# Output weights of four FFNs: their low halves from a negated copy and a transfer that adds, in place of a subtraction on VectorE

## The chip, the cores and the metric

The kernel runs on one core of one Trainium2 chip. Times are microseconds of device time of one execution of the whole program, and the median of several executions is compared. The profile is of one further execution.

## What is computed

A trunk of two layers over 256 context tokens and 512 latent tokens of width 1024. Each layer is a half-step SwiGLU FFN, a token mixer (differential attention in the first layer, grouped-query attention in the second) and another half-step FFN, each between two RMS norms and modulated by vectors that are made from the conditioning vectors `c` and `c_ctx`. The part that the change touches is the second matrix of the FFN, `w_out` of 2816 x 1024:

```python
def swiglu(h, w_in, w_out):
    gate, up = jnp.split(h @ w_in, 2, axis=-1)
    return (jax.nn.silu(gate) * up) @ w_out
```

All inputs are float32. The output is the latent stream, 512 x 1024.

## The kernel before, in words

**Products.** Every float32 operand is split in two float32r tiles: `hi` is a rounded copy (ScalarE, line 103, `nc.scalar.copy`), `lo` is what the rounding left, `src - hi` (VectorE, line 104). A product is three matmuls that add up in one PSUM bank: hi x hi, hi x lo, lo x hi. Weights come by a DMA on SyncE's queue into one of four `stage` buffers (line 129), and are split into a tile `wh` and a tile `wl`; there are six of each (`wtile`), used by all weights of the kernel.

**An FFN.** `ffn` runs four times: three times over all six tiles of 128 tokens ("wide"), and once over the four latent tiles. It first makes the 22 chunks of 128 columns of `silu(gate) * up`, each of which goes to DRAM (`gd`, line 468). In a wide FFN `chunk` does this with seven block products instead of eight, in an order of VectorE, ScalarE, GpSimd and TensorE that is written out by hand. Then comes w_out: `operand(c)` loads chunk c back (tile `gr`, or a `stage` buffer for the first three), splits it into `gx` tiles, and loads and splits the 128 x 1024 block c of `w_out`. The 22 operands are used in groups of 3, 3, 3, 3, 3, 2 and 5 (`GROUPS`): for each tile of tokens and each half of 512 columns, `project_half` runs three matmuls for each operand of the group into a bank `y_ps` (line 423; four banks), and `add_y` adds the bank to `y` in SBUF (ScalarE copies it for the first group, line 412; VectorE adds it after that, line 414). While one group runs, the operands of the next are made. The operands of the first group are made inside the last chunk of the first matrix (`prepare` and `finish_operands`, called by `chunk`). `w_out_last` runs the last group and, tile by tile, the norms that follow (`Finish`: GpSimd's lines 369, 97 and 99, VectorE's 382 and 388); there the order of VectorE, ScalarE and GpSimd is the program's.

**Beside it.** Between these steps, `Fillers` let VectorE make the modulation vectors of later layers from `ada_w` (lines 181 and 185), whose blocks also come through the `stage` buffers.

**What sets the order.** Outside of the orders written by hand, a planner sorts each engine's instructions before the program runs, by priority and by the time at which it expects operands and free tiles; that holds for TensorE in the whole of w_out, and for all engines in the groups but the last. On the chip each engine then runs its instructions in that order and waits where an operand is not there.

The names of the change: `operand` (line 670), `load_w` (line 112), which it called, `split` (line 102), `stage` and `wtile`.

Of the kernel before, what the change touches and what calls it, by code (L numbers as in the profile page):

```python
# [11 lines left out]
F32R = mybir.dt.float32r  # L12
AF = mybir.ActivationFunctionType
ALU = mybir.AluOpType
# [5 lines left out]
P = 128  # L20
D = 1024
# [38 lines left out]
def trunk(ctx: ExitStack, tc: tile.TileContext, a: dict, out: bass.AP):  # L60
    nc = tc.nc
# [40 lines left out]
    def split(hi, lo, src):  # L102
        nc.scalar.copy(hi, src)  # L103
        nc.vector.tensor_tensor(out=lo, in0=src, in1=raw(hi), op=ALU.subtract)  # L104

    def stage():
        return wp.tile([P, 1024], F32, tag="stage", name="stage", bufs=NSTAGE)

    def wtile(which):
        return wp.tile([P, 1024], F32R, tag="w" + which, name="w" + which, bufs=6)  # L110

    def load_w(src, dims, tiles=None):

        n = 1
        for d in dims:
            n *= d
        names = "abc"[: len(dims)]
        spec = {k: v for k, v in zip(names, dims)}

        def view(t):  # L120
            t = t[:, :n]
            return t.rearrange(f"p ({' '.join(names)}) -> p {' '.join(names)}", **spec) if len(dims) > 1 else t

        st = stage()
        if len(dims) == 3:
            for i in range(dims[0]):
                nc.sync.dma_start(out=view(st)[:, i], in_=src[:, i])
        else:
            nc.sync.dma_start(out=view(st), in_=src)
        hi, lo = tiles or (wtile("h"), wtile("l"))  # L130
        split(hi[:, :n], lo[:, :n], st[:, :n])
        return view(hi), view(lo)
# [310 lines left out]
    def ffn(ctx, l, s, tiles, place, fin, vectors, opening=None):  # L443
# [6 lines left out]
        w2 = a["ffn_w_out"][l, s]  # L450
# [205 lines left out]
        def two_tiles(which):  # L656
            if which == "k":
                return [ep.tile([P, 768], F32R, tag=f"kt{i}", name="gx", bufs=2) for i in range(2)]
            pool, n = (xp, 4) if which == "t" else (ep, 2)
            x = pool.tile([P, 2, 768], F32R, tag=which, name="gx", bufs=n)  # L660
            return x[:, 0, :], x[:, 1, :]
# [3 lines left out]
        def load_operand(c):  # L665
            r = stage() if c < GROUPS[0] else ep.tile([P, 768], F32, tag="pl", name="gr", bufs=4)
            nc.sync.dma_start(out=r[:, :nt], in_=gd[c])
            return r

        def operand(c, r=None):  # L670
            r = r or load_operand(c)
            gh, gl = two_tiles(next(slots))
            split(gh[:, :nt], gl[:, :nt], r[:, :nt])
            w = load_w(w2[c * P : (c + 1) * P, :], (D,))
            return (lambda t: gh[:, pos[t] : pos[t] + P], lambda t: gl[:, pos[t] : pos[t] + P]), w

        def w_out(ops, first):
# [29 lines left out]
        def prepare(n):  # L707
            if n < len(run):
                run[n].weights()
            else:  # L710
                rows.extend(load_operand(c) for c in range(2))
                ops.append(operand(0, rows[0]))
# [7 lines left out]
        def finish_operands(n):  # L720
            if n < len(run):
                run[n].summed()
            else:
                ops.append(operand(1, rows[1]))
                ops.extend(operand(c) for c in range(2, GROUPS[0]))
# [31 lines left out]
        if wide:  # L757
            run[0].load()
            with tc.manual_schedule(engines={ET.DVE, ET.Activation, ET.Pool, ET.PE}):
                evacuate(0, 0)  # L760
                nextp = [[bank("ff_ps2") for _ in range(2)] for _ in range(2)]
                for i in range(2):
                    for x in range(2):
                        wh, wl = nextw[x]
# [886 lines left out]
    with everything():  # L1651
# [5 lines left out]
        scale = ada_first(1, 0, stage)  # L1657
# [101 lines left out]
```

## Time and profile before

| | us |
|---|---|
| median of 3 runs | 2740.33 |
| lowest and highest | 2738.85 and 2741.08 |
| the profiled execution, whole | 2744.38 |
| its span, first to last instruction | 2742.6 |
| TensorE busy in it | 2639.0 (96%) |
| VectorE busy | 2016.4 (74%) |
| ScalarE busy | 1135.7 (41%) |
| GpSimd busy | 357.6 (13%) |

Engines are named PE (TensorE's products), PEld (its weight loads), DVE (VectorE), ACT (ScalarE), POOL (GpSimd) and SP (SyncE, which issues all DMAs); a "q" behind a name is the engine's queue. Line numbers are those of the kernel's file. A name such as `wl<-stage,wh` is the tile written and the tiles read. Matmuls are pipelined, so that one of 0.39 us follows the one before after 0.23 us.

### The profile page before, as it was taken

What the parts mean: (1) busy time and instruction counts of PE and PEld (TensorE: products, weight loads), DVE (VectorE), ACT (ScalarE), POOL (GpSimd) and SP (SyncE); (2) the same over time, 40 slices, a digit from 0 to 9 for tenths busy, and PEclk for the clock granted to TensorE, in tenths of its full rate; (3) what the DMA queues carried; (4) which work ended last, traced back from release to release, by engine and by line L of the source; (5) the groups of instructions that cost most, each with busy time, mean ns of one, the idle gap of its engine ahead of it and who ended that gap; (6) DMA issues with size and microseconds to landing.
All of it is one profiled execution on the core that took longest, in us unless ns stands there. A gap on an engine that the chain in (4) does not pass through costs nothing.

```text
span 2742.6 us, 38868 instructions
## 1 busy us (share of the span) xinstructions
PE 2639.0 (96%) x14720; PEld 2404.6 (88%) x14720; DVE 2016.4 (74%) x3052; ACT 1135.7 (41%) x2323; POOL 357.6 (13%) x643
## 2 busy tenths in 40 slices
PE   6999999989999998999999999999999999899998
PEld 5999998879999987999988789999787899788887
DVE  4988879867777787888788689787766778733355
ACT  4333333156666665333342353333324554622232
POOL 0000000054333343000000310000004210200001
PEclk9999999999999999999999999999999999999999
DMA  7444457531111113444375334344743211444452
GB/s 229 136 132 151 142 170 254 167 122 45 38 32 49 54 63 97 134 124 139 117 251 175 123 104 154 125 137 155 282 141 131 79 39 39 149 142 139 149 166 89
DMA packets 301860, 354.13 MB, mean 129 GB/s; under 512 B 15808, under 2 KB 234088, under 8 KB 301672
## 3 DMA queue, kind: packets, MB, share of 16 engines
q1 hardware_dynamic: 301672, 351.64, 39.9%
q8 instruction: 116, 1.90, 0.3%
q14 instruction: 72, 0.59, 0.1%
HBM read 303.05 MB, written 48.54 MB: 128 GB/s over the span
## 4 chain that ended last, share of the span: by engine, by line
PE 75%; DVE 9%; ACT 5%; issue 5%; POOL 3%; DMA 2%; POOLq 0%; DVEq 0%; ACTq 0%; SPq 0%
PE y_ps L423 23%; PE ff_p L615 15%; PE ff_ps L615 12%; PE ff_ps L735 8%; PE qkv_ps L806 5%; PE ff_ps L477 2%; PE ff_ps L767 1%; DVE h L382 1%; PE S L984 1%; DVE wl L104 1%; PE o_ps L1056 1%; ACT y L267 1%; PE kv_ps L806 1%; PE q_ps L806 1%; PE o_ps L1428 1%
## 5 line engine op out<-in xcount | busy, mean ns | idle before, releaser
L423 PE MATMUL y_ps<-wh,gx 128*128 128x512 f32 x1936 | 604.5, 391 | 1.5 <-ACT wh L103 1.5
L423 PEld LDWEIGHTS y_ps<-wh,gx 128*128 128x128 f32 x1936 | 363.2, 188 | 81.1 <-ACT wh L103 2.9
L103 ACT CAST wh<-stage 128x1024 fp32r<-128x1024 f32 x224 | 232.1, 1048 | 434.7 <-PE y_ps L423 217.0
L423 PE MATMUL y_ps<-wl,gx 128*128 128x512 f32 x968 | 377.3, 390 | 0.5 <-DVE wl L104 0.4
L104 DVE TENSOR_TENSOR wl<-stage,wh 128x1024 fp32r<-128x1024 f32 x224 | 273.2, 1224 | 96.3 <-ACT wh L103 94.4
L414 DVE TENSOR_TENSOR y<-y_ps,y 128x512 f32<-128x512 f32 x324 | 221.3, 686 | 109.3 <-PE y_ps L423 107.7
L369 POOL TENSOR_TENSOR yg<-y,g 128x512 f32<-128x512 f32 x44 | 58.3, 1326 | 1820.3 <-DVE y L414 1818.1
L185 DVE SCALAR_TENSOR_TENSOR acc<-stage,scond,acc 128x1024 f32<-128x1024 f32 x196 | 244.1, 1277 | 30.3 <-DMA stage<-in_ada_w 30.2
L615 PE MATMUL ff_p<-t,wh 128*128 128x384 f32 x960 | 244.4, 335 | 1.5 <-ACT sil L568 1.5
L103 ACT CAST wh<-raw 128x1024 fp32r<-128x1024 f32 x120 | 120.1, 1049 | 255.9 <-DVE raw L594 255.9
L423 PEld LDWEIGHTS y_ps<-wl,gx 128*128 128x128 f32 x968 | 181.8, 188 | 38.5 <-DVE wl L104 1.6
L615 PEld LDWEIGHTS ff_p<-t,wh 128*128 128x128 f32 x960 | 173.8, 188 | 1.8 <-ACT sil L568 1.8
L615 PE MATMUL ff_p<-t,wl 128*128 128x384 f32 x480 | 161.0, 335 | 2.9 <-DVE wl L104 2.9
L615 PE MATMUL ff_ps<-uh,wh 128*128 128x384 f32 x480 | 160.9, 335 | 1.7 <-DVE two L637 1.7
L615 PE MATMUL ff_ps<-uh,wl 128*128 128x384 f32 x480 | 160.4, 334 | 0.0
L615 PE MATMUL ff_ps<-ul,wh 128*128 128x384 f32 x480 | 160.3, 334 | 0.0
L104 DVE TENSOR_TENSOR wl<-raw,wh 128x1024 fp32r<-128x1024 f32 x120 | 141.2, 1218 | 0.0
L806 PE MATMUL qkv_ps<-wh,uh 128*128 128x384 f32 x384 | 136.9, 357 | 4.1 <-ACT wh L849 2.7
L806 PE MATMUL qkv_ps<-wl,uh 128*128 128x384 f32 x384 | 129.8, 338 | 2.5 <-DVE wl L852 2.5
L615 PE MATMUL ff_p<-uh,u 128*128 128x384 f32 x480 | 132.1, 336 | 0.0
L806 PE MATMUL qkv_ps<-wh,ul 128*128 128x384 f32 x384 | 129.9, 338 | 0.1
L615 PE MATMUL ff_ps<-t,wh 128*128 128x384 f32 x480 | 124.6, 340 | 2.2 <-ACT one L633 1.9
(250 smaller groups left out, 6356.4 us busy)
## 6 DMA issues: line engine op xcount, KB each, us to landing
stage<-in_ffn_w_in SPq DMA_DIRECT2D x176, 512.0 KB
stage<-in_ada_w SPq DMA_DIRECT2D x136, 512.0 KB
stage<-in_ffn_w_out SPq DMA_DIRECT2D x88, 512.0 KB
gd<-g SPq DMA_DIRECT2D x66, 384.0 KB
gr<-gd SPq DMA_DIRECT2D x57, 384.0 KB
stage<-in_da_w_in SPq DMA_DIRECT2D x64, 192.0 KB
hd<-h SPq DMA_DIRECT2D x18, 512.0 KB
h<-hd SPq DMA_DIRECT2D x16, 512.0 KB
```

The costliest lines, as they stand in the source:

```text
L103: nc.scalar.copy(hi, src)
L104: nc.vector.tensor_tensor(out=lo, in0=src, in1=raw(hi), op=ALU.subtract)
L185: nc.vector.scalar_tensor_tensor(out=acc[c], in0=st, scalar=scond[:, k, c : c + 1], in1=acc[c], op0=ALU.mult, op1=ALU.add)
L267: nc.scalar.activation(junk, src, AF.Square, accum_out=ss)
L369: nc.gpsimd.tensor_tensor(out=self.yg[:, cols], in0=ys[t][:, cols], in1=self.gate[1 if t < CT else 0][:, cols], op=ALU.mult)
L382: nc.vector.scalar_tensor_tensor(out=h, in0=yg, scalar=r, in1=h, op0=ALU.mult, op1=ALU.add)
L414: nc.vector.tensor_tensor(out=y, in0=ps, in1=y, op=ALU.add)
L423: nc.tensor.matmul(ps, lhsT=x, rhs=w, start=(i == 0), stop=(i == n - 1))
L477: nc.tensor.matmul(ps, lhsT=ww[:, k, :], rhs=moving(uu, k, two), start=(k == 0 and n == 0), stop=(k == KC - 1 and n == 2),)
L615: nc.tensor.matmul(ps[:, :hw], lhsT=ww[:, k * P : (k + 1) * P], rhs=bb[:, k, cols], start=(first and k == 0 and n == 0), stop=(last and k ...
L735: nc.tensor.matmul(ps[:, :nt], lhsT=ww[:, k, :], rhs=uu[:, :, k, cols], start=(k == 0 and n == 0), stop=(k == KC - 1 and n == 2),)
L806: nc.tensor.matmul(ps[:, :n], lhsT=x, rhs=w, start=(k == 0 and m == 0), stop=(k == KC - 1 and m == 2))
```

## The change

The block of `w_out` is loaded into a `stage` buffer as before and rounded to `wh`. Then ScalarE writes `-wh` into `wl`, and GpSimd issues a DMA that adds the same block of `w_out`, read from DRAM a second time, to `wl`. VectorE's subtraction for this weight is left out. `load_w` stays as it is for all other weights.

```diff
@@ -671,7 +671,14 @@
             r = r or load_operand(c)
             gh, gl = two_tiles(next(slots))
             split(gh[:, :nt], gl[:, :nt], r[:, :nt])
-            w = load_w(w2[c * P : (c + 1) * P, :], (D,))
+            st = stage()
+            src = w2[c * P : (c + 1) * P, :]
+            nc.sync.dma_start(out=st, in_=src)
+            wh, wl = wtile("h"), wtile("l")
+            nc.scalar.copy(wh, st)
+            nc.scalar.activation(wl, wh, AF.Copy, scale=-1.0)
+            nc.gpsimd.dma_start(out=wl, in_=src.bitcast(F32R), accum_op=ALU.add)
+            w = wh, wl
             return (lambda t: gh[:, pos[t] : pos[t] + P], lambda t: gl[:, pos[t] : pos[t] + P]), w
```

## Rows read from the trace of the kernel before

**Rows 1.** The page: each engine's busy us (share of the span) and instructions
```profile
PE 2639.0 (96%) x14720; PEld 2404.6 (88%) x14720; DVE 2016.4 (74%) x3052; ACT 1135.7 (41%) x2323; POOL 357.6 (13%) x643
```

**Rows 2.** Four w_out stretches: us, engines' busy us (instructions), clock, DMA share, GB/s
```profile
393.90:537.80 143.90, 143.56 (x665) 115.86 (x664) 133.35 (x153) 43.04 (x54) 0.00 (x0) 1.00 0.69 226
1393.10:1535.30 142.20, 141.75 (x648) 115.60 (x647) 115.81 (x137) 40.97 (x53) 0.00 (x0) 1.00 0.62 206
1920.30:2062.40 142.10, 140.89 (x636) 114.32 (x636) 100.77 (x124) 41.08 (x53) 0.00 (x0) 1.00 0.61 208
2614.00:2707.00 93.00, 93.00 (x416) 76.42 (x416) 57.31 (x77) 30.35 (x44) 0.00 (x0) 1.00 0.46 146
sum 521.20, PE 519.21 PEld 422.21 DVE 407.25 ACT 155.45 POOL 0.00; mean PE 129.80 PEld 105.55 DVE 101.81 ACT 38.86 POOL 0.00
```

**Rows 3.** TensorE's waits: who waited for whom, us in total, times, longest
```profile
PE pre_t L280 <- DVE y L388: 13.2, 12, 1.7
...
PE y_ps L423 <- ACT wh L103: 1.5, 2, 1.2
...
PE y_ps L423 <- DVE wl L104: 0.4, 1, 0.4
```

**Rows 4.** The page's groups: line engine op, count, busy us, mean ns, idle before
```profile
L103 ACT CAST wh<-stage 128x1024 fp32r<-128x1024 f32 x224 | 232.1, 1048 | 434.7 <-PE y_ps L423 217.0
...
L104 DVE TENSOR_TENSOR wl<-stage,wh 128x1024 fp32r<-128x1024 f32 x224 | 273.2, 1224 | 96.3 <-ACT wh L103 94.4
```

**Rows 5.** Timeline of ScalarE, then VectorE, 1467 to 1476: start, us, instruction [idle before]
```profile
1467.70 2.00 ACT L103 CAST wh<-stage 128x1024 fp32r<-128x1024 f32 x2 [21.07 <-PE y_ps L423]
...
1474.32 1.22 DVE L104 TENSOR_TENSOR wl<-stage,wh 128x1024 fp32r<-128x1024 f32 x1
```

**Rows 6.** Timeline of GpSimd, 1512 to 1545: its first instruction there
```profile
1539.84 1.28 POOL L369 TENSOR_TENSOR yg<-y,g 128x512 f32<-128x512 f32 x1 [474.51 <-DVE y L414]
```

**Rows 7.** The page's queue of data, and the chain's pieces that are landings (start, us)
```profile
q1 hardware_dynamic: 301672, 351.64, 39.9%
...
383.56 5.26 DMA stage<-in_ffn_w_out
391.32 4.22 DMA stage<-in_ffn_w_out
...
595.28 2.82 DMA stage<-in_da_w_in
...
1389.21 3.76 DMA stage<-in_ffn_w_out
...
1917.56 5.07 DMA stage<-in_ffn_w_out
```

**Rows 8.** Timelines of ScalarE, VectorE, TensorE at the start of the second w_out
```profile
1384.91 1.05 ACT L103 CAST wh<-stage 128x1024 fp32r<-128x1024 f32 x1 [0.76 <-DMA stage<-in_ffn_w_out]
...
1393.00 1.05 ACT L103 CAST wh<-stage 128x1024 fp32r<-128x1024 f32 x1 [5.90 <-DMA stage<-in_ffn_w_out]
...
1394.08 1.23 DVE L104 TENSOR_TENSOR wl<-stage,wh 128x1024 fp32r<-128x1024 f32 x1 [2.89 <-ACT wh L103]
...
1395.36 0.50 PE L423 MATMUL y_ps<-wl,gx 128*128 128x512 f32 x1 [0.45 <-DVE wl L104]
```

**Rows 9.** Timelines at the last group: second FFN: ScalarE, then VectorE
```profile
1534.93 2.01 ACT L103 CAST wh<-stage 128x1024 fp32r<-128x1024 f32 x2 [13.84 <-PE y_ps L423]
...
1535.61 0.69 DVE L414 TENSOR_TENSOR y<-y_ps,y 128x512 f32<-128x512 f32 x1 [0.67 <-PE y_ps L423]
1536.22 2.35 DVE L104 TENSOR_TENSOR wl<-stage,wh 128x1024 fp32r<-128x1024 f32 x2
1539.01 0.69 DVE L414 TENSOR_TENSOR y<-y_ps,y 128x512 f32<-128x512 f32 x1 [0.44 <-PE y_ps L423]
```

**Rows 10.** Timeline of TensorE at the start of the third w_out
```profile
1920.29 0.39 PE L423 MATMUL y_ps<-wh,gx 128*128 128x512 f32 x1
...
1923.75 0.74 PE L423 MATMUL y_ps<-wh,gx 128*128 128x512 f32 x2 [1.21 <-ACT wh L103]
```

## The prediction

> **What bounds the kernel now.** I read first the busy shares of the page, then the four stretches in which the output weights are used, then TensorE's waits there, and last the instructions around the two kinds of places where a weight comes late. TensorE is busy for 96% of the span [rows 1]. [...] The same is seen from the waits: products of `y_ps` stood still for 1.9 us in the whole kernel, at three places, before a `wh` or a `wl` [rows 3]. So w_out is bound by TensorE, the subtraction on VectorE is beside it, and what the change can do there is to take away 1.9 us or to add waits.
>
> **What is removed.** 88 of the 224 subtractions `wl<-stage,wh` (one for each of 22 output weights in four FFNs), 1.224 us each [rows 4]: 88 x 1.224 = 108 us of VectorE. On the path to the end: none of it but the wait of 0.4 us on `wl` [rows 3], because TensorE has work behind it. What is late next is TensorE itself.
>
> **What is added, off the path.** ScalarE makes the negated copy: same shape and width as the cast `wh<-stage`, 1.048 us [rows 4], so 88 x 1.05 = 92 us. ScalarE's queue has room: it is busy for 155.45 us of the four stretches [rows 2], and idles for 21.07 us before it makes the weights of a next group [rows 5]. The last `wl` of such a group is made some 8 us after the group before has let the tiles go (1467.70 to 1475.5) and needed one group of 108 products later, at 1492, so 16 us are left [rows 5]; one more copy for each of three weights (3.2 us) and a transfer fit there. That cover serves 18 of the 22 weights of an FFN (all but those of the first group and the last one of all); I cost them at nothing, and if three transfers together took over some 13 us it would be gone. Queued behind a negated copy on ScalarE are in the first group the evacuations of `y_ps`, which have four banks and so three halves of slack. GpSimd issues 88 transfers, and waits at each for ScalarE; behind it stands nothing, since in the second FFN its first instruction after 474.51 us of idling comes at 1539.84, 2.8 us behind the last add that it would issue (1537.0) [rows 6]. SyncE's queue gets no new instruction, and the stage buffer is free one subtraction earlier, when ScalarE has read it. The stretches move 146 to 226 GB/s at a DMA share of 0.46 to 0.69 [rows 2]; 22 weights of 0.52 MB are 11.5 MB more, in 93 to 144 us some 80 to 124 GB/s.
>
> **What is added, on the path: the price of one transfer that adds.** The trace has no DMA issued by GpSimd and none that adds; all its data packets go through one hardware queue [rows 7]. Bounds: below, the shortest of the loads that the chain names, 2.82 us for one of 192 KB; above, twice the longest load of an output weight, 5.26 us, so 10.5 us [rows 7]. The four loads of an output weight on the chain took 5.26, 4.22, 3.76 and 5.07 us, 4.6 in the mean [rows 7]. An add reads the destination as well as the source. Taking 2.82 us for what doesn't grow with the bytes, the moving part is 4.6 - 2.82 = 1.8 us, and twice that makes X = 2.82 + 3.6 = 6.4 us, nearest to the rows of the same tensor. I take 6.4, and an excess over a plain load of 1.8.
>
> [...]
>
> **Place A, the step from the products of the first matrix to w_out (three wide FFNs).** In the second FFN the load of the third output weight is issued at 1389.21 [rows 7], when VectorE has let go of a stage buffer; the cast runs from 1393.00, the subtraction from 1394.08 to 1395.31, and TensorE, at the product that needs it, starts at 1395.36 after 0.45 us of waiting [rows 8]. With the change: cast to 1394.05, negated copy to 1395.1, add to 1401.5, that is 6.2 us later. Where the load can take the buffer that ScalarE's cast of 1384.91 now frees at 1385.96 instead [rows 8], it is 3.2 us earlier, 3.0 us later in all. So 3.0 to 6.2 us for each of three places if TensorE's order stays, middle 4.6.
>
> **Place B, the fifth weight of the last group (all four FFNs).** Groups of 2 and 5 need seven weights and there are six tiles, so the fifth waits for the group of two. In the second FFN ScalarE's cast starts at 1534.93, when TensorE lets the tile go; the two subtractions start at 1536.22, the first is ready at 1537.4; the first half of the last group is added at 1539.01, so its low product, the last but one of 15, began one product (0.39 us) and one step (0.23 us) earlier, at 1538.4 [rows 9]. Slack 1.0 us. The pattern stands four times, once in each FFN. With the change: 1534.93 + 1.05 + 1.05 + 6.4 = 1543.4, which is 5.0 us behind 1538.4. Four places: 20 us.
>
> **What TensorE can do meanwhile.** Its order in w_out is the planner's, and the planner does move products: in the third FFN products of w_out run from 1920.29, and the wait of 1.21 us ends at 1923.75, so the last one before it began by 1922.15 and nine ran, where the first half has six for the two weights at hand; three are of the other half [rows 10]. At 0.227 us a product (15 of them from 1535.61 to 1539.01 [rows 9]) three more halves of 12 products cover 3 x 2.7 = 8.2 us at B, and at A the other half's six products cover 1.4 us and two more banks as they come free another 2.7. That covers X = 6.4 at B, and most of it at A, if the planner expects the add as late as it comes. What it expects too early stays as a wait: on plain loads it was off by 1.9 us over three places, 1.2 at worst [rows 3]. I let it expect the add like a plain load of the same size and so be 1.8 us short at each place: 7 x 1.8 = 12.6, less the 1.9 that stood there before, + 10.7 us.
>
> **The sum** is made against the profiled execution, a span of 2742.6 us in a run of 2744.38; the median of the runs is 2740.33, which is 4.05 us or 0.15% less. 2744.4 + 10.7 = 2755.1 profiled, 2751.0 by the median.
>
> **Rivals.**
> 1. Covered: the planner places TensorE's products behind the adds, or X is near 3 us. Then the seven places cost 0 to 0.6 each (as the 1.9 over three do now): 2738 to 2743, no change. For it: the order in [rows 10]; against: the same order left 1.21 us.
> 2. The order stays: 3 x 4.6 + 20 - 1.9 = + 32 us, 2772. For it: in the second FFN w_out runs from 1393.1 [rows 2] and the last product before the wait began by 1394.5 [rows 8], so seven ran, the six of two weights and the third weight's own first: no other half was moved ahead. Against it: [rows 10].
> 3. DMA becomes the bound. At 226 GB/s for a share of 0.69, 80 GB/s more are 0.25 as a copy and 0.49 if an add costs twice: 1.18 in the first stretch, 1.11 and 1.10 in the next two, 0.46 + 0.78 = 1.24 in the fourth. If TensorE pays all of it: 26 + 16 + 14 + 22 = + 78 us, 2818. It decides from a share of 1. Against it: part of the traffic are loads for VectorE's fillers, which can slip.
> 4. Faster: VectorE's queue is the mechanism. In the tails of the FFNs TensorE waits 13.2 us in 12 pieces for `y` (L388) [rows 3]; a subtraction less in front of each of four last groups gives back at most 4 x 1.22 = 4.9, and with the 1.9 at A it is 6.8 us: 2733.5. It needs X under some 2.5 us or a full cover, and VectorE late at those places, where it idles 0.44 us [rows 9].
>
> **How the numbers follow.** Forecast (waits of 1 to 3 us at most of the seven places, 2746 to 2760) 0.37; covered 0.28; the order stays, wholly or in part (2760 to 2790) 0.19; DMA-bound 0.08; faster 0.08. The range leaves out half of the fastest case and what lies over 2790: 2736 to 2790. A measurement here tells some 0.2% (5.5 us) from no change: faster than 2734.9 in 0.08, within in 0.30 (covered, and 0.02 of the forecast's low end), slower in 0.62.
>
> **What would show it.** Subtractions `wl<-stage` on VectorE fall by 88 and its busy time by 108 us; ScalarE's rises by 92. Waits of `y_ps` on a DMA of `wl` appear near the seven places and sum to some 12 us; a sum near 0 is rival 1, over 25 rival 2. A DMA share near 1 in w_out with waits spread over all groups is rival 3. Landings of the add at 3 or 10 us make X wrong; an order of TensorE without other halves ahead of the wait makes the cover wrong.

## The result, and the profile after

The changed kernel took 2825.43 us (median of 4 runs, 2821.91 to 2827.64), the kernel before 2740.70 beside it: a ratio of 1.0309 with a 95% interval of 1.0291 to 1.0327. It is 85 us slower; the forecast was 2751, and its range ended at 2790. The two profiled executions lie 79.3 us apart (spans of 2821.9 and 2742.6).

The page's first rows of the profiled execution after (2823.62 us, span 2821.9), then its two queues of data (packets, MB, share of 16 engines), the chain, and the line on the added transfer (its last number is the median us from issue to landing):

```profile
PE 2662.2 (94%) x14720; PEld 2414.6 (86%) x14720; DVE 1922.6 (68%) x2964; ACT 1218.6 (43%) x2411; POOL 434.2 (15%) x731
...
q1 hardware_dynamic: 301672, 351.64, 38.2%
q0 software_dynamic: 12672, 46.14, 8.7%
...
PE 63%; DVE 10%; issue 9%; DMA 8%; ACT 6%; POOL 4%; SPq 0%; DVEq 0%; POOLq 0%; ACTq 0%
...
wl<-in_ffn_w_out POOLq DMA_DIRECT2D x88, 512.0 KB, 8.9
```

Beside [rows 1], VectorE has its 88 instructions less (3052 to 2964) and is busy for 93.8 us less, not for the 108 that were forecast; ScalarE has 88 more. TensorE has the same 14720 products, but they take 23.2 us longer. There is a second queue of data, q0. 46.14 MB of it take 8.7% of the DMA engines' time, 0.189% for a MB; on q1 a MB takes 0.109%. So a byte that is added costs 1.74 times what a loaded byte costs.

Where the time went is seen with TensorE's w_out stretches taken whole, from the first product to the end of the last. First the kernel before, then after (us, busy us of each engine (instructions), granted clock, DMA share, GB/s; the sum line stands last):

```profile
393.90:585.30 191.40, 188.78 (x879) 153.11 (x878) 162.90 (x192) 63.25 (x89) 24.58 (x31) 1.00 0.61 199
...
sum 692.30, PE 683.40 PEld 557.18 DVE 508.19 ACT 219.02 POOL 85.94; mean PE 170.85 PEld 139.29 DVE 127.05 ACT 54.75 POOL 21.48
```

```profile
391.80:613.00 221.20, 198.28 (x879) 158.14 (x879) 142.03 (x172) 82.16 (x110) 42.11 (x51) 0.95 0.76 223
1418.70:1636.40 217.70, 194.28 (x861) 156.78 (x860) 123.30 (x151) 77.85 (x106) 42.58 (x51) 0.96 0.71 208
1974.00:2187.70 213.70, 196.29 (x856) 157.37 (x855) 108.52 (x141) 79.19 (x107) 42.67 (x51) 0.96 0.74 216
2690.20:2813.90 123.70, 121.26 (x537) 98.81 (x535) 49.90 (x72) 51.00 (x67) 26.25 (x30) 1.00 0.77 202
sum 776.30, PE 710.11 PEld 571.09 DVE 423.74 ACT 290.21 POOL 153.60; mean PE 177.53 PEld 142.77 DVE 105.94 ACT 72.55 POOL 38.40
```

The four stretches grew from 692.30 to 776.30 us, by 84.0: the whole loss is there, and the rest of the span is 4.7 us shorter (79.3 - 84.0). The loss has two parts. TensorE stands still, in what are called holes below, for 776.30 - 710.11 = 66.2 us instead of 8.9, which is 57.3 more. And the same products take 710.11 us instead of 683.40, 26.7 more, with a granted clock of 0.95 to 0.96 in the three wide FFNs, where it was 1.00: 5, 4 and 4% of these stretches are an estimated 28 us.

TensorE's waits after (us in all, times, longest), which answer [rows 3]:

```profile
PE y_ps L423 <- DMA wl<-in_ffn_w_out: 44.5, 16, 6.8
PE y_ps L423 <- DVE y L414: 14.6, 6, 4.7
```

In the kernel before the first was not there and the second was 0.2 us. The first is the added transfer landing late. Where it stands is seen in TensorE's timeline of the first FFN (start, us, instruction, [idle before and what ended it]), of which the six waits for an add are shown, and two pairs of other products for the step between them:

```profile
397.51 0.79 PE L423 MATMUL y_ps<-wl,gx 128*128 128x512 f32 x1 [4.63 <-DMA wl<-in_ffn_w_out]
...
404.28 1.05 PE L423 MATMUL y_ps<-wh,gx 128*128 128x512 f32 x2
...
408.49 0.50 PE L423 MATMUL y_ps<-wl,gx 128*128 128x512 f32 x1 [1.51 <-DMA wl<-in_ffn_w_out]
...
410.21 0.62 PE L423 MATMUL y_ps<-wh,gx 128*128 128x512 f32 x2
...
430.50 0.50 PE L423 MATMUL y_ps<-wl,gx 128*128 128x512 f32 x1 [2.68 <-DMA wl<-in_ffn_w_out]
434.07 0.79 PE L423 MATMUL y_ps<-wl,gx 128*128 128x512 f32 x1 [2.61 <-DMA wl<-in_ffn_w_out]
...
437.85 0.79 PE L423 MATMUL y_ps<-wl,gx 128*128 128x512 f32 x1 [1.27 <-DMA wl<-in_ffn_w_out]
...
569.66 0.80 PE L423 MATMUL y_ps<-wl,gx 128*128 128x512 f32 x1 [5.00 <-DMA wl<-in_ffn_w_out]
```

397.51 and 408.49 stand at the step that the prediction calls place A; the first of them waits for the second weight, and the prediction had only the third there. 569.66 is place B. The three between them are the three weights of the second group, a place that the prediction did not have. Two products with a step between them take 1.05 us at 404.28 and 0.62 at 410.21: the step is 0.43 us instead of 0.23. Three windows of the same execution, around the holes and between them, show why (columns as above):

```profile
395.10:405.20 10.10, 6.57 (x15) 4.69 (x16) 6.05 (x7) 2.89 (x4) 0.86 (x1) 0.50 0.79 249
405.40:432.00 26.60, 21.87 (x94) 17.13 (x93) 14.17 (x13) 16.48 (x24) 2.63 (x3) 1.00 0.91 294
432.70:442.80 10.10, 7.45 (x17) 5.38 (x18) 2.27 (x4) 4.01 (x6) 1.77 (x2) 0.50 1.04 319
```

Around the holes of 4.63 and 2.61 us the granted clock is 0.50, and in between it is 1.00. In the w_out stretches of the kernel before it was 1.00 in every window of 1 us.

The second line of waits has another cause. VectorE's timeline in the third FFN, after, at the longest of them:

```profile
2055.86 1.28 DVE L185 SCALAR_TENSOR_TENSOR acc<-stage,scond,acc 128x1024 f32<-128x1024 f32 x1 [7.71 <-DMA stage<-in_ada_w]
2057.06 1.28 DVE L414 TENSOR_TENSOR y<-y_ps,y 128x512 f32<-128x512 f32 x2
```

A filler stands ahead of the sums on VectorE and waits 7.71 us for its block of `ada_w`; the sum behind it, which lets a bank of `y_ps` go, comes when four banks are full, and TensorE waits 4.67 us. Before the fillers of line 185 VectorE waited 64.7 us in all for `ada_w`, in the kernel before 30.2.

So two theories had to be told apart. **Late add:** the transfer lands too late for the product that needs it, at places with little slack, whatever else is moving. **Crowding:** 46 MB more at 1.74 times the price delay all loads, and the waits follow from that.

### The profile page after: what moved, and what is told of

It reads as the page before. It is cut to its first block, busy times and chain, and to the rows that moved or that the text cites. A ratio compares the mean times of both kernels' runs of the same rounds, so it can differ in the third digit from the quotient of the medians.

```text
span 2821.9 us, 39124 instructions
## 1 busy us (share of the span) xinstructions
PE 2662.2 (94%) x14720; PEld 2414.6 (86%) x14720; DVE 1922.6 (68%) x2964; ACT 1218.6 (43%) x2411; POOL 434.2 (15%) x731
## 3 DMA queue, kind: packets, MB, share of 16 engines
q1 hardware_dynamic: 301672, 351.64, 38.2%
q0 software_dynamic: 12672, 46.14, 8.7%
## 4 chain that ended last, share of the span: by engine, by line
PE 63%; DVE 10%; issue 9%; DMA 8%; ACT 6%; POOL 4%; SPq 0%; DVEq 0%; POOLq 0%; ACTq 0%
PE y_ps L423 15%; PE ff_p L615 14%; PE ff_ps L615 11%; PE ff_ps L742 8%; PE qkv_ps L813 5%; DMA stage<-in_ada_w 3%; DMA wl<-in_ffn_w_out 2%; PE ff_ps L477 2%; DVE acc L185 1%; DMA gr<-gd 1%; DMA stage<-in_ffn_w_out 1%; PE ff_ps L774 1%; DVE h L382 1%; PE S L991 1%; DVE wl L104 1%
## 5 line engine op out<-in xcount | busy, mean ns | idle before, releaser
L423 PE MATMUL y_ps<-wh,gx 128*128 128x512 f32 x1936 | 620.8, 400 | 15.6 <-DVE y L414 14.4
L423 PEld LDWEIGHTS y_ps<-wh,gx 128*128 128x128 f32 x1936 | 373.8, 193 | 101.0 <-DVE y L414 18.4
L423 PE MATMUL y_ps<-wl,gx 128*128 128x512 f32 x968 | 387.4, 400 | 44.5 <-DMA wl<-in_ffn_w_out 44.5
L680 POOL DMA_DIRECT2D wl<-in_ffn_w_out x88 | 77.9, 885 | 1758.5 <-ACT wl L679 644.2
L185 DVE SCALAR_TENSOR_TENSOR acc<-stage,scond,acc 128x1024 f32<-128x1024 f32 x196 | 244.8, 1279 | 64.7 <-DMA stage<-in_ada_w 64.7
L104 DVE TENSOR_TENSOR wl<-stage,wh 128x1024 fp32r<-128x1024 f32 x136 | 166.5, 1228 | 71.2 <-ACT wh L103 69.7
```

What stands on the lines that cost most here:

```text
L185: nc.vector.scalar_tensor_tensor(out=acc[c], in0=st, scalar=scond[:, k, c : c + 1], in1=acc[c], op0=ALU.mult, op1=ALU.add)
L423: nc.tensor.matmul(ps, lhsT=x, rhs=w, start=(i == 0), stop=(i == n - 1))
L680: nc.gpsimd.dma_start(out=wl, in_=src.bitcast(F32R), accum_op=ALU.add)
```

## Experiments

Times stand beside runs of the kernel before that were made with them (2739.7 to 2740.4 us). Diffs are against the changed kernel.

**1. The negated copy without the transfer.** The sum is left out, so `wl` holds `-wh`.

```diff
-            nc.gpsimd.dma_start(out=wl, in_=src.bitcast(F32R), accum_op=ALU.add)
```

> The changed kernel without its transfer: ScalarE writes the negated copy, nothing is added to it, so the low halves of the output weights are wrong. If the loss comes from the transfer (late adds, or the crowding of the DMA engines by it): no wait of TensorE on wl in w_out, VectorE relieved by 108 us, 2736 to 2742 us. If it comes from the rest of the change (the extra ScalarE copies, the planner's new order): the loss stays, 2800 to 2830.

2742.31 us, ratio 1.0011 (1.0001 to 1.0020), within 0.3 us of the first expectation. VectorE is rid of 88 subtractions, ScalarE makes its 88 copies, and nothing is won: the w_out stretches take 693.4 us. The whole loss comes with the transfer.

**2. A plain copy by GpSimd instead of copy and add.** `wl` is overwritten with the block; nothing is subtracted.

```diff
-            nc.scalar.activation(wl, wh, AF.Copy, scale=-1.0)
-            nc.gpsimd.dma_start(out=wl, in_=src.bitcast(F32R), accum_op=ALU.add)
+            nc.gpsimd.dma_start(out=wl, in_=src.bitcast(F32R))
```

> GpSimd's transfer copies the block into wl instead of adding it, and ScalarE's negated copy is left out, so wl holds the weight itself and the output is wrong. The same bytes are read from DRAM, but nothing is read back from SBUF. If adding is what makes the transfer slow, its landing falls from a median of 8.9 us to 5 or 6 and the time to 2750 to 2775. If it is GpSimd's issue or the second reading of the weights, landings stay near 8 to 9 us and the time at 2800 to 2825.

2763.18 us, 1.0080 (1.0063 to 1.0097). The copy waits for no other step, can start with the load of the same block, and lands after 6.0 us; products waited 2.1 us for it. What they waited for was the upper half, 12.1 us before `wh` and 6.4 before VectorE's sums. The longest of these, 7.7 us at the start of the first w_out, stands behind ScalarE, which had waited 8.22 us for the load of that block. The DMA engines were 0.96 busy in that hole (392.30 to 400.50): that fits copies which start with the loads and share the engines with them, though no run takes the two apart. The two data queues of this kernel, which give a plain copied MB 0.111% of the engines' time, as much as a loaded one:

```profile
q1 hardware_dynamic: 301672, 351.64, 38.7%
q0 software_dynamic: 12672, 46.14, 5.1%
```

So a second transfer of the blocks costs 23 us where it runs beside the loads of the same weights, by these waits, which fit crowding, and the price of 1.74 belongs to adding.

**3. The adds onto tiles that nobody reads.** VectorE subtracts as before; 88 adding transfers go to DRAM.

```diff
-            nc.scalar.activation(wl, wh, AF.Copy, scale=-1.0)
-            nc.gpsimd.dma_start(out=wl, in_=src.bitcast(F32R), accum_op=ALU.add)
+            nc.vector.tensor_tensor(out=wl, in0=st, in1=raw(wh), op=ALU.subtract)
+            unused = dr.tile([P, 1088], F32, name="unused", tag="unused", bufs=4)[:, :1024]
+            nc.gpsimd.dma_start(out=unused, in_=src, accum_op=ALU.add)
```

> The low halves by VectorE's subtraction as before, and beside it the same 88 adding transfers of 512 KB from GpSimd, to tiles in DRAM that nobody reads. Late adds as the cause: nobody waits for them, 2738 to 2748 us. Crowding of the DMA engines as the cause: the blocks of ada_w and of the next weights come late all the same, DMA share in w_out 0.8 to 0.9, 2780 to 2825.

2878.93 us, 1.0508 (1.0490 to 1.0526). This run doesn't test what it was made for. An add without an operand to wait for is free to go early, and the planner put 22 adds into the first 250 us of the program, beside the loads of the first matrix, the first at 41.35. These 250 us (columns as above), then those of the changed kernel:

```profile
0.00:250.00 250.00, 192.39 (x1105) 175.24 (x1106) 152.86 (x232) 84.95 (x144) 25.05 (x44) 0.89 0.67 184
```

```profile
0.00:250.00 250.00, 225.01 (x1343) 209.06 (x1344) 195.75 (x284) 98.45 (x166) 6.71 (x22) 0.97 0.52 166
```

TensorE is busy for 33 us less there, and in the whole kernel it waited 45.6 us for ScalarE's step `one` in the first matrices. It was made again, with a GpSimd copy of one column that reads `wh` ahead of each add. It takes 0.93 us, about as long as the negated copy (1.06 us) that the changed kernel's add waits for, so each add is issued about when the changed kernel would issue it (lines added to the edit above, around its transfer):

```diff
+            after = sm.tile([P, 1], F32, tag="after", name="after")
+            ins = nc.gpsimd.tensor_copy(after, raw(wh)[:, :1])
+            with tc.issue_after(ins.ins):
+                nc.gpsimd.dma_start(out=unused, in_=src, accum_op=ALU.add)
```

> VectorE subtracts as in the kernel before, and each block is beside that added by a transfer onto DRAM tiles that nothing reads. A GpSimd copy of one column that reads the upper half of the weights goes ahead of each add, so that the adds are issued where the changed kernel issues them. Late add: nobody waits for these transfers, so 2738 to 2748. Crowding: the traffic is that of the changed kernel or more, so most of the loss is there, 2780 to 2830, with the loads of the fillers and of the conditioning weights late, and VectorE's work that waits for them.

2779.47 us, 1.0142 (1.0127 to 1.0157): just under what crowding expected, and far from what a late add alone allows. TensorE waited 16.1 us for VectorE's sums, and VectorE 63.3 us for `ada_w`, as in the changed kernel. But this kernel has all of VectorE's 108 us of subtractions, which the changed one hasn't, so its queue is longer, and by the program its adds go to tiles in DRAM where the changed kernel's go to the tile on the chip. Its 39 us say what crowding can cost, not what it costs there.

**4. The changed kernel without most of what the adds crowd.** The fillers' loads of `ada_w` carry 128 of 1024 columns, and VectorE's instructions keep their sizes (the first of the two pieces of the edit; the second lets them read the 128 columns repeatedly).

```diff
+            if vector:
+                nc.sync.dma_start(out=st[:, :P], in_=a["ada_w"][l, k * P : (k + 1) * P, v * D : v * D + P])
+                return st[:, :P].rearrange("p (o n) -> p o n", o=1).to_broadcast([P, KC, P])
```

> The changed kernel with the fillers' loads of the conditioning weights cut to 128 of their 1024 columns (an eighth of the bytes; VectorE's instructions keep their sizes, and what they compute from these columns is left out). Crowding: with the fillers' loads gone from beside them the adds land in 5 to 6 us instead of 8.9 and most of the loss goes, 2740 to 2765. Late add by itself: an add still lands some 6 us after its issue or later and most of the loss stays, 2790 to 2825.

> Control: the kernel before with the same cut of the fillers' loads (the same part of the computation is left out). Its TensorE stretches wait for almost nothing that these loads delay, so 2725 to 2742 by either theory.

2809.61 us for the changed kernel with the cut, 2738.19 for the kernel before with it: 71.4 us are left of 85. The waits of the first:

```profile
PE y_ps L427 <- DMA wl<-in_ffn_w_out: 43.8, 14, 7.0
PE y_ps L427 <- DVE y L418: 5.5, 4, 3.5
```

The waits for sums fall from 14.6 to 5.5 us, which is the crowding. Those for the add stay at 43.8, and it lands after 5.4, 8.7 and 12.9 us (least, median, most), where it landed after 5.5, 8.9 and 12.8: the length of an add does not come from the bytes of the fillers' loads. So some 13 us of 85 come from these bytes, which is a lower bound on the crowding: VectorE still waits 57.9 us for the cut blocks (17.6 in the control), and 5.5 us of waits for sums are left. The other 71 us are left without them: the late add, the clock after its holes, and what crowding remains.

**5. What makes an add long.** Once it takes its operand from the stage tile on the chip instead of DRAM, once it carries a single column.

```diff
-            nc.gpsimd.dma_start(out=wl, in_=src.bitcast(F32R), accum_op=ALU.add)
+            nc.gpsimd.dma_start(out=wl, in_=st.bitcast(F32R), accum_op=ALU.add)
```

> The add takes its operand from the stage tile on the chip, where the first transfer has put it, instead of reading the block of the output weights from DRAM a second time. If the reading of 46 MB more from DRAM is what costs, about half of the loss or more goes: 2740 to 2785. If what costs is how late the add itself lands, the landing stays near 9 us and the time near that of the changed kernel, 2810 to 2835; it can also be longer, since the stage tile is held until the add has landed and the next load of its buffer waits for that.

```diff
-            nc.gpsimd.dma_start(out=wl, in_=src.bitcast(F32R), accum_op=ALU.add)
+            nc.gpsimd.dma_start(out=wl[:, :1], in_=src[:, :1].bitcast(F32R), accum_op=ALU.add)
```

> The adding transfer carries one column of the 1024 (128 elements of 4 bytes, 0.5 KB instead of 512 KB); the rest of the sum is left out. Issue, queue, write and wait stay, the bytes go. If the fixed part of an added transfer makes the weights late (issue on GpSimd, its queue, the notice of its end), it still lands 4 us or more after its issue and the loss is half or more of 85 us: 2780 to 2815. If the bytes make it late, it lands some 2 to 3 us after its issue, within the slack at nearly all places, and the time is 2742 to 2755.

From the stage tile: 2831.99 us, 1.0337 (1.0322 to 1.0352), slower still, although the add landed after 6.9 us in the median. TensorE waited 49.3 us for it, up to 8.7, and 20.2 for sums. The loss does not need the second reading of DRAM. What that reading costs by itself is not shown, because this run has a delay of its own: by the program a stage buffer is now held until its add has landed, and there are four. One column: 2761.15 us, 1.0078 (1.0063 to 1.0093). It landed after 4.3 us in the median, as the first expectation had it, but the time lies between the two; products waited 11.0 us for it. From issue to landing:

| transfer on GpSimd's queue | least | median | most | against before |
|---|---|---|---|---|
| add, one column (0.5 KB) | 2.2 | 4.3 | 7.7 | + 21 us |
| plain copy, 512 KB | 3.6 | 6.0 | 13.3 | + 23 us |
| add from the stage tile, 512 KB | 4.5 | 6.9 | 11.7 | + 92 us |
| add from DRAM, 512 KB (changed kernel) | 5.5 | 8.9 | 12.8 | + 85 us |

An estimate from the least values: some 2.2 us come with the transfer of one column, 1.4 more with the bytes (3.6 - 2.2) and 1.9 more with adding them (5.5 - 3.6). The medians lie 2 to 3.4 us above; three adds issued one behind the other, as at 420.42, 424.02 and 426.39, let their products go after some 10, 10 and 11.5 us.

**6. The number of adds or their place.** Three kernels add at some blocks and subtract on VectorE at the others.

```diff
-            nc.scalar.activation(wl, wh, AF.Copy, scale=-1.0)
-            nc.gpsimd.dma_start(out=wl, in_=src.bitcast(F32R), accum_op=ALU.add)
+            if 9 <= c < 17:
+                nc.scalar.activation(wl, wh, AF.Copy, scale=-1.0)
+                nc.gpsimd.dma_start(out=wl, in_=src.bitcast(F32R), accum_op=ALU.add)
+            else:
+                nc.vector.tensor_tensor(out=wl, in0=st, in1=raw(wh), op=ALU.subtract)
```

> Negated copy and adding transfer for blocks 9 to 16 of each feed-forward network alone (32 of 88); VectorE subtracts the other 56. If the loss comes from the weights that TensorE wants soon after the start and at the end of a stretch (late add), it goes nearly whole: 2738 to 2748. If it comes from the traffic of the adds beside the other loads (crowding), it goes with the number of adds: 32 of 88 of 85 us, some 31 us, so 2765 to 2780. The holes that stand between the first and second group of the changed kernel are partly inside these blocks, so a late add alone can leave up to some 10 us.

With `if c < 9 or c == 21` in its place:

> Negated copy and adding transfer for blocks 0 to 8 and 21 of each feed-forward network (40 of 88), the places where TensorE stood still in the changed kernel; VectorE subtracts the other 48. Late add: nearly all of the loss of the changed kernel stays, less what its 48 other adds cost (blocks 9 to 16 alone cost 8 us): 2800 to 2820. If the loss goes with the number of adds, 40 of 88 of 85 us: 2775 to 2785.

With `if c == 21`:

> Negated copy and adding transfer for block 21 alone, the last weight of each feed-forward network (4 of 88); VectorE subtracts the other 84. In the changed kernel TensorE stood still for 5.0, 4.5, 3.6 and 2.2 us before these four, 15.3 us, with the clock lower after each. If what decides is the place of a late add and not the number of adds, these four cost the holes and about half as much again at the lower clock, 15 to 24 us: 2755 to 2764. With nothing else in the queue beside it an add can land nearer to 5.5 us than to 8.9, so 3 us less at each place, and then 8 to 12 us: 2748 to 2752. If the cost goes with the number of adds, it is 4 us: 2744.

| adds at blocks | adds | us | against before | ratio, interval |
|---|---|---|---|---|
| 9 to 16 | 32 | 2748.74 | + 8.3 | 1.0033 (1.0020 to 1.0046) |
| 0 to 8 and 21 | 40 | 2810.77 | + 71.1 | 1.0257 (1.0240 to 1.0275) |
| 21 | 4 | 2760.11 | + 20.4 | 1.0070 (1.0056 to 1.0084) |

The first two kernels have about as many adds, and in the first they even take longer (10.4 us in the median against 8.2), yet it loses a ninth of what the second loses. Four adds alone cost 20.4 us. TensorE's timeline at these four, and GpSimd's issue of the first of them:

```profile
547.31 0.80 PE L423 MATMUL y_ps<-wl,gx 128*128 128x512 f32 x1 [4.97 <-DMA wl<-in_ffn_w_out]
```

```profile
539.07 1.08 POOL L681 DMA_DIRECT2D wl<-in_ffn_w_out  x1 [498.19 <-DVE wl L862]
```

With no other add beside it, this one was issued at 539.07 and let TensorE go on at 547.31, 8.2 us later. The holes of the four are 5.0, 3.9, 4.1 and 2.2 us, 15.2 in all. Over the w_out stretches TensorE idles 13.7 us more than before, and its products take 8.0 us longer, with granted clocks of 0.98 and 0.99. It is the place that decides.

**7. The subtraction on GpSimd.** The same relief of VectorE without a transfer.

```diff
-            nc.scalar.activation(wl, wh, AF.Copy, scale=-1.0)
-            nc.gpsimd.dma_start(out=wl, in_=src.bitcast(F32R), accum_op=ALU.add)
+            nc.gpsimd.tensor_tensor(out=wl, in0=st, in1=raw(wh), op=ALU.subtract)
```

> The subtraction of the output weights on GpSimd instead of VectorE, with no second transfer: VectorE is relieved as in the changed kernel. By twice the 1.33 us of GpSimd's 128x512 product a subtraction takes 2.7 us, so the fifth weight of the last group is ready 0.2 us late. If relief of VectorE is worth anything in w_out: 2730 to 2736. If w_out is TensorE's alone: 2738 to 2744.

2774.82 us, 1.0128 (1.0112 to 1.0143), outside both expectations. GpSimd needs 2757 ns for each, products waited 5.1 us for it, 6.5 for upper halves and 12.4 for VectorE's sums, and VectorE wins nothing: it has 88 instructions less and is busy for 2014.4 us where it was 2016.4. Its other instructions got longer. One group of instructions, first before, then in this kernel:

```profile
L185 DVE SCALAR_TENSOR_TENSOR acc<-stage,scond,acc 128x1024 f32<-128x1024 f32 x196 | 244.1, 1277 | 30.3 <-DMA stage<-in_ada_w 30.2
```

```profile
L185 DVE SCALAR_TENSOR_TENSOR acc<-stage,scond,acc 128x1024 f32<-128x1024 f32 x196 | 276.4, 1442 | 42.6 <-DMA stage<-in_ada_w 42.3
```

The splits of loaded chunks (`gx<-gr,gx`, 128x768) went from 950 to 1547 ns. In this kernel's first FFN, VectorE's instructions of the group just ahead of a GpSimd subtraction and beside it, a sum beside it, and the subtraction:

```profile
460.94 1.27 DVE L185 SCALAR_TENSOR_TENSOR acc<-stage,scond,acc 128x1024 f32<-128x1024 f32 x1
...
462.74 2.82 DVE L185 SCALAR_TENSOR_TENSOR acc<-stage,scond,acc 128x1024 f32<-128x1024 f32 x1
465.48 0.68 DVE L414 TENSOR_TENSOR y<-y_ps,y 128x512 f32<-128x512 f32 x1
...
461.60 2.87 POOL L679 TENSOR_TENSOR wl<-stage,wh 128x1024 fp32r<-128x1024 f32 x1 [19.81 <-ACT wh L678]
```

None of these kernels with the change or a part of it is faster than the one before.

## Why the prediction was wrong, and where it was right

**Right: what bounds w_out, and that the relief is worth nothing.** The first experiment has the removal alone and stays at 2742.31 us; so the 1.9 us could not be had either. ScalarE's 88 copies hid, as costed. The direction and the mechanism (waits of `y_ps` on the DMA of `wl`, by places) were forecast as well; their number, their length and what follows a wait were not.

**The sum, term by term.** The forecast was 7 x 1.8 = 12.6 us of waits at places A and B, less 1.9, and nothing else. Measured, of the 84.0 us in the w_out stretches: 33.6 of waits for the add at the two places (18.3 at A, 15.3 at B: 5.0, 4.5, 3.6 and 2.2), 10.9 of waits for it elsewhere, nearly all in the second group, 12.8 net of other waits (sums behind fillers, above all), and 26.7 of slower products. So four steps failed: the cover that left 1.8 us at each place, the nothing for the 18 other weights, the nothing for VectorE's sums behind fillers that wait for late loads, and the missing price of a hole.

**The first of these: 18 of 22 weights at nothing.** The slack of 16 us was read at one boundary, between two groups of three in the middle of an FFN [rows 5], and was given to every group but the first and the last. It holds for the middle: 32 adds at blocks 9 to 16 cost 8.3 us. It doesn't hold for the second group, blocks 3 to 5. In the kernel before, the first of these subtractions and the product that needs its result stand as follows (VectorE, then TensorE):

```profile
417.20 1.21 DVE L104 TENSOR_TENSOR wl<-stage,wh 128x1024 fp32r<-128x1024 f32 x1
...
419.59 0.39 PE L423 MATMUL y_ps<-wl,gx 128*128 128x512 f32 x1
```

Ready at 418.41, needed at 419.59: 1.2 us of slack, not 16. In the second FFN the third weight of this group had 5 us (ready at 1414.9, needed at 1419.97). These rows were in the trace of before and were not read. In the changed kernel no product waits more than 0.2 us for an add between the second group and the last weight, so from the third group on there is slack enough.

**The price of an add, X, was too small.** 6.4 us was taken from bounds of 2.82 to 10.5; the median is 8.9, the least 5.5. The idea that an add moves twice the bytes was near (1.74 times a load in engine time), but it was set on a fixed part of a load on SyncE's queue. From the four loads of an output weight [rows 7], 4.6 us in the mean, to a copy of the same block on GpSimd's queue, 6.0 in the median, it is 1.4 us more, and the row for that wasn't in the trace of before.

**Place B was right in its rival and wrong in the forecast.** The working had a weight 5.0 us late at each of four places, 20 us, and then took most of it back, because the planner would move three halves of products ahead (8.2 us of cover) and expect the add only 1.8 us too early. The last experiment measures this place by itself: holes of 5.0, 3.9, 4.1 and 2.2 us. The planner did move products: 24, 26, 26 and 23 of the last group ran before the hole, where the first half has 14 without this weight. That is 9 to 12 of another half, 2.0 to 2.7 us at 0.227 each, and not 8.2. What is left open at each place is 2.2 to 5.0 us and not 1.8. Nothing in the trace of before said what the planner takes an add for; the 1.8 was an assumption from plain loads. That the first hole is 5.0, the number of the working without cover, is luck: from the release of the tile (536.01) to the product (547.31) it took 11.3 us and not 8.5, and the products moved ahead gave some of that back.

**Rival 2 (the order stays) named the places but not their number or what follows.** Its waits for the add, 3 x 4.6 + 20 = 33.8 us, are the 33.6 measured at A and B, but partly by luck: it had 4.6 at each A for the third weight alone, and measured were, for the second and the third weight, 4.63 and 1.51 in the first FFN, 1.64 and 6.84 in the second, 3.20 and 0.49 in the third. At B it had 20 where 15.3 were measured. With the second group this makes 16 waits and 44.5 us; the forecast had 7 and 12.6.

**Not in any term: the lower clock.** 26.7 of the 84 us are the same products at a lower granted clock. The w_out of before could not show it, since no product there waited for more than 1.2 us [rows 3]. But the same trace shows it elsewhere, where TensorE goes on to the mixer after the third FFN (its timeline, then a window around the wait, columns as above):

```profile
2117.23 0.58 PE L806 MATMUL kv_ps<-wl,uh 128*128 128x256 f32 x1 [2.57 <-DVE wl L104]
```

```profile
2116.00:2120.00 4.00, 2.77 (x13) 2.77 (x14) 4.00 (x5) 3.62 (x7) 2.15 (x1) 0.50 0.41 122
```

A rival with holes of 3 to 6 us needed a price for what comes after them, and this was a row to take it from.

**Rival 3 (DMA-bound, 2818) came nearest to the number, by the wrong mechanism.** It wanted DMA shares of 1.1 to 1.24 and waits in all groups. The shares of the whole stretches are 0.71 to 0.77, and the waits for the add stand in the first two groups and at the last weight; only in short windows is the share near 1 (1.04 from 432.70 to 442.80). Its term for a second reading at twice the price was near (1.74). What the prediction held against it, that loads for fillers can slip, held in part: they slipped, and their bytes cost some 13 us all the same.

**The sum as it should have stood:** 44.5 us of holes for the add, 12.8 of other waits, 26.7 for the clock, 84.0 in all.

**What stays open.** Why an add takes 8.9 us in the median and 5.5 at the least is known by steps (table above), but what lies between the least and the median of a one-column add, 2.2 and 4.3 us, is not separated. The split of 71 and 13 us rests on cutting one kind of load; other loads stayed, and so did the other adds beside each add.

## What to carry to other kernels

Read slack at every place where the operand is used, the second group after a change of stage among them, and not at one boundary; here a step that got 5 to 9 us longer cost what the places with the least slack lacked. The latency that was moved from an engine to a transfer was paid where the weights are late, not in proportion to their number: 4 of 88 cost a quarter of the loss. Where the relieved engine isn't the bound, test the relief by itself first; here it was worth nothing (2742.31 us beside 2739.85).

## What the hardware showed that was not expected

**A hole of TensorE cost about half as much again, in nine of ten kernels.** Summed over the four w_out stretches, against the kernel before:

| kernel | idle more, us | busy more, us |
|---|---|---|
| changed | 57.3 | 26.7 |
| add from the stage tile | 66.4 | 28.9 |
| changed, fillers' loads cut | 49.8 | 22.4 |
| blocks 0 to 8 and 21 | 45.2 | 24.3 |
| block 21 | 13.7 | 8.0 |
| blocks 9 to 16 | 6.7 | 3.0 |
| one column | 12.9 | 7.2 |
| plain copy | 18.5 | 7.4 |
| subtraction on GpSimd | 22.4 | 11.2 |
| unread adds, in place | 18.1 | 19.8 |

The first nine lie between 0.40 and 0.58 us of slower products for a us of idling, with the traffic of the adds, with next to none of it (one column) and with none at all (GpSimd). So in these runs it goes with the holes and not with the transfers. The last one doesn't fit: its granted clock is 1.00, 0.99, 0.98 and 1.00 in the four stretches, which is an estimated 6 of its 19.8 us, and what the others are is open. No run took the clock apart by itself.

**A MB that was added in a transfer took 1.74 times the engine time of a loaded MB** (8.7% for 46.14 MB against 38.2% for 351.64), **and one that was copied on the same queue 1.00 times** (5.1% against 38.7% for the same bytes). What of the 1.74 is reading and what is adding, no run shows.

**GpSimd's subtraction slowed VectorE:** 1277 to 1442 ns in the mean for the group shown and 2.82 us for one that ran beside it, so that 88 instructions taken from VectorE left its busy time where it was. The sums `y<-y_ps,y` were not slowed (686 and 684 ns).
